# Two unused tiles in SBUF shift the first bytes of a float32r network's weights and activations

## The chip, the core and the metric

The kernel runs on one NeuronCore of a Trainium2 chip. What counts is the device time of one execution in microseconds (us). In the profile PE is TensorE's matmul row, PEld its weight load, DVE VectorE, ACT ScalarE, POOL GpSimd and SP SyncE, whose queue issues the DMAs.

## The reference

One sequence of 256 tokens with 1,024 features goes through two blocks, all in float32. The first block is a feed forward, a hybrid mixer (attention with a forget gate beside a gated delta rule), an attention over a memory of 256 tokens, and a second feed forward. The second block has two layers, each of a feed forward, a mixer (a gated short convolution beside a state space scan), a feed forward and a gated embedding. Cut to what most of the time goes into:

```python
def rms_norm(x, gain):
    xf = x.astype(jnp.float32)
    y = xf * lax.rsqrt(jnp.mean(xf * xf, axis=-1, keepdims=True) + EPS)
    return (y * gain.astype(jnp.float32)).astype(x.dtype)

def swiglu(x, w_gate, w_up, w_down):          # [256,1024] @ [1024,2816], and back
    return (jax.nn.silu(x @ w_gate) * (x @ w_up)) @ w_down

f = swiglu(rms_norm(h, ffn1_pre_norm[l]), ffn1_w_gate[l], ffn1_w_up[l], ffn1_w_down[l])
h = h + FFN_RESIDUAL_WEIGHT * rms_norm(f, ffn1_post_norm[l])
mixed = hybrid_mixer(rms_norm(h, mix_pre_norm[l]), w_in[l], ...)
h = h + rms_norm(mixed @ w_out[l], mix_post_norm[l])
...
return rmsnorm(h, final_norm)
```

There are six such feed forwards and about as much again in the mixers' projections. Each weight is read from memory once.

## The kernel before

**Tiling.** Activations lie with features on the 128 partitions and the 256 tokens along the free axis. A weight unit is 128 partitions by up to four row chunks of 256 columns. It is taken by `wunit` (L283): one DMA into `raw` (L296), a rounding copy into `hi` on ACT (L297), and the remainder into `lo` on DVE (L298). These are tiles of [128, 1024] float32 (4,096 bytes a partition) in the pool `wp`: four buffers of `raw`, three each of `hi` and `lo`.

**The products.** An activation is likewise kept as two float32r parts in one tile `r` of [128, 2, 256] (2,048 bytes a partition). A product of one weight chunk with one activation chunk is three matmuls (`mm3`): hi with the high part, hi with the low part, lo with the high part. Each is a matmul of 256 moving columns with its own load of 128 columns of weights, issued by `mm` at L265. In the profile `pm<-r,hi` means: into a PSUM tile `pm`, the moving operand from an `r` tile, the weights from a `hi` tile. Where weights were loaded ahead (`preload`) they lie in `r` tiles too, and the row reads `pm<-r,r`; where tokens are to stand on the partitions (`proj_tok`) the parts change places, and it reads `pm<-hi,r`. `px<-r,smw` is a product with a few columns of weights (32 or 64 of 128) from a tile `smw`. Matmuls of plain float32 on small tiles are `px<-con,rk` (the identity in `con` moves; the weights are one column of `rk`, repeated), `px<-d,s` and `px<-s,d`; `px<-con,s` at L268 are transposes.

**Order.** A scheduler puts the instructions in order when the program is built; weight units are taken `AHEAD` = 60 places early.

**Where tiles lie.** A pool's tiles are laid one behind another in SBUF, rounded up to 32 bytes, pool after pool: `cst` (constants), `wp` (weights), `sc` (scratch: `sq`, `acc`, `rb`, `t`, `w`, small vectors), `arena` (36 tiles `s` of [128, 256] float32, 20 tiles `r`), and behind these the tiles of a part of the network (`scope`: more `r`, `s` and `d` tiles, 22 `r` tiles in a feed forward). All tiles of `wp` and `arena` have sizes that are multiples of 1,024 bytes, so one pool's tiles all begin at the same remainder of 128, and so do the slices of 512 or 1,024 bytes that matmuls read of them. The pools are opened at L145 to L149, and `mhalf` at L170 is the last constant that is laid down before the products begin.

Of the kernel before, what the change touches and what calls it, by code (L numbers as in the profile page):

```python
# [8 lines left out]
F32 = mybir.dt.float32  # L9
# [6 lines left out]
P = 128  # L16
S = 256
D = 1024
KC = D // P
# [4 lines left out]
# columns of the packed per-feature vectors (one column per 128 features)  # L24
# [10 lines left out]
# rows that every partition holds  # L35
# [54 lines left out]
# how many places of the program order a weight unit is taken ahead, how many one that preload() takes,  # L90
# and how many places products that wait for other engines are put back
# [5 lines left out]
class Arena:  # L97
    """fixed tiles, handed out and taken back in program order"""
# [6 lines left out]
    def add(self, pool, n):  # L105
        """n more tiles from pool, which are handed out first"""
        new = []
        for _ in range(n):
            nm = f"{self.name}{self.n}"
            new.append(pool.tile(self.shape, self.dtype, tag=nm, name=nm, bufs=1)[:])  # L110
            self.n += 1
        self.free[:0] = new
        self.parts.append(new)
# [7 lines left out]
    def get(self, keep=False):  # L121
        """keep: a tile that outlives the parts added last"""
        n = len(self.parts[-1]) if keep and len(self.parts) > 1 else 0
        late = {id(t) for t in self.parts[-1]} if n else ()
        k = [i for i, t in enumerate(self.free) if id(t) not in late]
        assert k, f"arena {self.name} is full"
        t = self.free.pop(k[0])
        self.used[id(t)] = t
        self.peak = max(self.peak, len(self.used))
        return t  # L130
# [6 lines left out]
class Net:  # L137
    def __init__(self, ctx, tc, a):
        self.tc, self.nc, self.a = tc, tc.nc, a
        nc = self.nc  # L140

        def pool(name, bufs, **kw):
            return ctx.enter_context(tc.tile_pool(name=name, bufs=bufs, **kw))

        self.cst = pool("cst", 1)  # L145
        self.wp = pool("wp", 3)
        self.scr, self.parts, self.pp = {}, [], []
        self.sc = pool("sc", 2)
        ap = pool("arena", 1)  # L149
        self.S = Arena("s", [P, S], F32)  # L150
        self.S.add(ap, 36)
        self.R = Arena("r", [P, 2, S], F32R)
        self.R.add(ap, 20)
        self.D = Arena("d", [P, 2, S], F32)
        self.D.add(ap, 0)
        self.pm = pool("pm", 4, space=bass.MemoryType.PSUM)
        self.px = pool("px", 4, space=bass.MemoryType.PSUM)

        self.con = self.cst.tile([P, NCON], F32, name="con")
        self.vec = self.cst.tile([P, NPACK], F32, name="vec")  # L160
        self.ones = {n: self.cst.tile([P, 1], F32, name=f"ones{n}") for n in (1, 128, 512, 1024)}
        nc.gpsimd.memset(self.ones[1], 1.0)
        for n in (128, 512, 1024):
            self.act(self.ones[n], self.ones[1], AF.Copy, scale=1.0 / n)
        self.h = self.start()
        self.ident = self.c("ident")
        nc.sync.dma_start(self.ident, a["con"][:, :P])
        self.ones_sq = self.cst.tile([P, P], F32, name="ones_sq")
        nc.gpsimd.memset(self.ones_sq, 1.0)
        self.mhalf = self.cst.tile([P, 16], F32, name="mhalf")  # L170
        nc.gpsimd.memset(self.mhalf, -0.5)

    def constants(self):
# [7 lines left out]
        # masks and selectors, exact in bfloat16  # L181
# [11 lines left out]
    def start(self):  # L193
        """the activations in the order that the first products need them, with the first weights between"""
# [30 lines left out]
    def t(self, tag, shape, dtype=F32, bufs=2, part=False):  # L225
        """scratch: the next of bufs fixed tiles; part: only there within the current scope"""
        pool, scr = self.parts[-1] if part else (self.sc, self.scr)
        if tag not in scr:
            scr[tag] = [[pool.tile(shape, dtype, tag=f"{tag}{i}", name=f"{tag}{i}", bufs=1)
                         for i in range(bufs)], 0]  # L230
        r = scr[tag]
        r[1] += 1
        return r[0][r[1] % len(r[0])][:]

    def half(self):
        """scratch [P, 256]: halves of the two t tiles in turn"""
# [11 lines left out]
    def late(self, *names):  # L248
        """products that wait for other engines, put behind others that are ready"""
        return self.tc.high_priority(-sum(LATE[n] for n in names))  # L250
# [32 lines left out]
    def wunit(self, src, a, prio=True, cut=1):  # L283
        """hi/lo parts of src [P, a, 256], in cut pieces"""
# [3 lines left out]
        n = a * S  # L288
# [13 lines left out]
    def first(self, *src):  # L302
        """the units that come first when the first blocks of src are taken in step"""
        return [(q, 0, ks) for ks in self.steps(KC) for q in src]

    def preload(self, *units):
        """the parts of units (src, block, row chunks), which are the next to be used, in tiles of the arena"""
# [10 lines left out]
    def units(self, src, b, K):  # L318
        """the weight units of column block b of src [blocks, P, K, 256]: row chunks, hi/lo parts"""
# [13 lines left out]
    def steps(K):  # L333
        """the row chunks of each weight unit"""
        return [range(k, min(k + 4, K)) for k in range(0, K, 4)]

    def block(self, src, b, x, banks):
        """two out chunks in step, so that each weight unit is used up at once"""
# [7 lines left out]
    def proj(self, src, b0, nblk, x, evict, wide=False, last=False):  # L346
        """evict(chunk, ps) with ps [P, 256]: out features on partitions; wide: the first two blocks in step;
        last: the chunks of the last block one after the other"""
# [20 lines left out]
    def proj_tok(self, src, b0, nblk, x, evict):  # L369
        """evict(blk, t, ps) with ps [P, 256]: tokens of tile t on partitions"""  # L370
# [19 lines left out]
    def sq_acc(self, acc, src):  # L390
        """acc + src*src for src [P, 256] (acc None to begin)"""
# [7 lines left out]
    def rstd(self, acc, n, mult=1.0):  # L399
        """[P tokens, 2] of (mean + eps)^-1/2 / sqrt(mult) from tiles of squares or a pair of means in PSUM"""  # L400
# [15 lines left out]
    def spread(self, r, cols=(0, 1)):  # L416
        """PSUM [P, 256]: token values r[:, cols] along the free axis, same on every partition"""
# [21 lines left out]
    def sum_squares(self, ps, h, c):  # L439
        """mean square of the chunks, summed by the tensor engine"""  # L440
# [17 lines left out]
    def scope(self, r, d, s):  # L458
        """more tiles for one part of the network: r float32r pairs, d float32 pairs, s singles"""
# [48 lines left out]
    def residual(self, h, scale):  # L508
        """evict that adds scale*ps to h in place"""
# [4 lines left out]
    def post(self, gain, mult):  # L514
        """evict that keeps gain*f and the squares; then finish adds the normalised f to h"""
# [14 lines left out]
        def finish(h, gain):  # L530
            """also returns the parts of gain*h and the squares for the norm that follows"""
# [13 lines left out]
    def softplus(self, x, shape):  # L545
        """x is a small SBUF tile; returns log(1 + exp(x))"""
# [19 lines left out]
    def three(self, ps, n, tag):  # L566
        """bf16 tile [96, n]: the float32 rows of ps (three copies of 32) in three exact parts"""
# [12 lines left out]
    def small_cols(self, src, n, x, rb=None):  # L580
        """token-major [P, 2, n] of x (times rb) by the few columns of src [P, KC, n]"""
# [3 lines left out]
        # both parts of the columns side by side  # L585
# [22 lines left out]
    def conv(self, y, x, taps, K):  # L608
        """y = causal convolution of x [P, 256] with K taps (columns), bias already folded by the caller"""
# [4 lines left out]
    def mixer1(self, h, x, acc):  # L614
# [55 lines left out]
        # k normalised  # L670
# [17 lines left out]
        # token-major gates  # L688
# [40 lines left out]
        # output norm and gate of the delta rule heads  # L729
# [26 lines left out]
    def gdn(self, kq, vT, g, beta, nbeta):  # L756
        """the outputs, their mean squares, and what runs the delta rule for a few heads"""
# [19 lines left out]
        def run(heads):  # L777
            for hd in heads:
# [22 lines left out]
                # token-major keys and values  # L801
# [12 lines left out]
                # the strictly lower part takes the place of the keys  # L814
# [6 lines left out]
                # q scaled by its decay, in place  # L821
# [85 lines left out]
    def fox(self, fq, fk, fvt, nls):  # L907
# [10 lines left out]
        def run(hd, out):  # L918
            """head hd, split into its half of out"""
# [67 lines left out]
    def mem_attn(self, x, acc):  # L987
# [11 lines left out]
        def weights(hd):  # L999
            """softmax of the head's scores, transposed: [P memory, 2, 256 tokens]"""  # L1000
# [47 lines left out]
    def mixer2(self, h, i, pool):  # L1048
# [39 lines left out]
        # gated short convolution  # L1088
# [76 lines left out]
    def ssd(self, sm, xbc, L):  # L1165
# [28 lines left out]
        def decay(grp, c):  # L1194
            """cb times the decay within the chunks for a pair of heads, transposed"""
# [78 lines left out]
    def ple_proj(self, i):  # L1274
        """the embeddings' part, which no activation comes into"""
# [133 lines left out]
def _arrays(inputs):  # L1409
    """the inputs laid out for the chip: feature-major activations, small vectors packed by partition"""  # L1410
# [22 lines left out]
    def blocks(w):  # L1433
        """[..., K, N] as [..., N/256, P, K/P, 256]: one run of memory per partition and column block"""
# [40 lines left out]
```

## Time and profile before

| | us |
|---|---|
| runs | 2216.78, 2227.3, 2217.13 |
| median of the runs | 2217.13 |
| span of the profiled execution | 2217.7 |

The span runs from the first to the last instruction of the one execution that was profiled. The runs are whole executions; the profiled one has no run time of its own beside its span, which lies 0.6 us above the median. PE is busy for 99% of the span, PEld for 97%, DVE for 70%, ACT for 53%, and the 16 DMA engines for 53%. A busy PE says little by itself, because matmuls overlap each other: how far apart they start is what shows the pace, that is the length of a stretch divided by the matmuls in it.

### The profile page before, as it was taken

The page shows a single profiled execution, that of the slowest core. Times are in us where ns is not written, and L with a number is a line of the kernel's source. Part 1 is how long each engine was busy: PE and PEld are TensorE (multiplying, and loading weights), DVE is VectorE, ACT ScalarE, POOL GpSimd, SP SyncE. Part 2 cuts the span into 40 slices and gives each one's busy share as a digit, 9 for nine tenths or more (in the row PEclk, how much of TensorE's full clock was granted, in tenths as well). Part 3 has the DMA queues.
Part 4 walks back from the last instruction along what each step waited for, and adds up shares of the span by engine and source line. Part 5 has one row for each costly group of instructions (what it writes and reads, how often), then busy time and mean ns, then how long its engine had stood idle before and what let it go on. Part 6 is the DMA issues. An engine that isn't in the chain of part 4 may idle for free.

```text
span 2217.7 us, 45480 instructions
## 1 busy us (share of the span) xinstructions
PE 2195.2 (99%) x18672; PEld 2152.2 (97%) x18672; DVE 1558.5 (70%) x2608; ACT 1185.1 (53%) x2033; POOL 43.3 (2%) x54
## 2 busy tenths in 40 slices
PE   8999999999999999999999999999999999999998
PEld 8999997999999999998999999999999999999998
DVE  6756873667665766798766766676669886767666
ACT  6545633555454544567555554454457755645444
POOL 0000000000000000000000000000000000000000
PEclk9999997999999999999999999999999999999999
DMA  7565520435556556553455556655665436555563
GB/s 255 177 185 169 166 77 1 166 121 162 189 184 191 173 188 186 186 186 106 157 189 185 192 190 195 190 182 195 190 196 187 136 125 193 179 193 193 193 188 127
DMA packets 110369, 379.44 MB, mean 171 GB/s; under 512 B 12368, under 2 KB 17104, under 8 KB 110160
## 3 DMA queue, kind: packets, MB, share of 16 engines
q1 hardware_dynamic: 110160, 376.53, 52.9%
q8 instruction: 146, 2.39, 0.4%
q14 instruction: 63, 0.52, 0.1%
HBM read 375.43 MB, written 1.05 MB: 170 GB/s over the span
## 4 chain that ended last, share of the span: by engine, by line
PE 95%; DVE 2%; ACT 1%; DMA 1%; issue 0%; POOL 0%; SPq 0%; DVEq 0%; ACTq 0%; POOLq 0%
PE pm L265 84%; PE px L265 11%; PE px L268 1%; DVE lo L298 1%; DVE s L259 0%; DMA raw<-in_ffn_w_up_dram 0%; DMA raw<-in_ple_w_gate_dram 0%; ACT hi L297 0%; DMA raw<-in_ffn_wu_dram 0%; DVE r L259 0%; ACT d L262 0%; PE pm L268 0%; ACT L262 0%; DVE acc L256 0%; DVE w L253 0%
## 5 line engine op out<-in xcount | busy, mean ns | idle before, releaser
L265 PE MATMUL pm<-r,hi 128*128 128x256 f32 x10640 | 1861.5, 279 | 7.2 <-ACT hi L297 5.7
L265 PEld LDWEIGHTS pm<-r,hi 128*128 128x128 f32 x10640 | 1621.7, 189 | 9.5 <-ACT hi L297 5.7
L265 PE MATMUL pm<-r,lo 128*128 128x256 f32 x5320 | 1484.4, 279 | 1.6 <-DVE lo L298 1.6
L298 DVE TENSOR_TENSOR lo<-raw,hi 128x1024 fp32r<-128x1024 f32 (+1 forms) x718 | 861.0, 1200 | 488.3 <-ACT hi L297 484.4
L297 ACT CAST hi<-raw 128x1024 fp32r<-128x1024 f32 (+1 forms) x718 | 739.1, 1030 | 731.5 <-PE pm L265 576.5
L265 PEld LDWEIGHTS pm<-r,lo 128*128 128x128 f32 x5320 | 1001.4, 188 | 3.2 <-DVE lo L298 2.2
L276 ACT CAST r<-w 128x256 fp32r<-128x256 f32 x136 | 54.5, 403 | 61.0 <-DVE w L253 61.0
L253 DVE TENSOR_TENSOR t<-pm,rb 128x512 f32<-128x512 f32 (+1 forms) x132 | 80.4, 636 | 0.2
L262 ACT ACTIVATE r<-s,vec 128x256 fp32r<-128x256 f32 x136 | 66.1, 504 | 22.1 <-DVE s L259 18.2
L262 ACT ACTIVATE sq<-s 128x256 f32<-128x256 f32 x152 | 60.3, 410 | 27.6 <-DVE s L253 19.8
L259 DVE SCALAR_TENSOR_TENSOR s<-pm,vec,s 128x255 f32<-128x255 f32 x144 | 68.9, 479 | 2.8
L259 DVE SCALAR_TENSOR_TENSOR r<-s,vec,r 128x256 fp32r<-128x256 f32 x136 | 65.5, 499 | 5.0 <-ACT r L262 4.4
L265 PE MATMUL px<-r,hi 128*128 128x256 f32 x384 | 66.9, 279 | 0.0
L277 DVE TENSOR_TENSOR r<-w,r 128x256 fp32r<-128x256 f32 x136 | 57.0, 422 | 8.1
L265 PEld LDWEIGHTS px<-r,hi 128*128 128x128 f32 x384 | 58.5, 189 | 0.0
L265 PE MATMUL px<-r,lo 128*128 128x256 f32 x192 | 53.5, 278 | 0.0
L413 POOL TENSOR_TENSOR rs<-rv,mhalf 128x2 f32<-128x2 f32 x26 | 23.4, 898 | 1504.2 <-DVE rv L411 1504.2
L262 ACT ACTIVATE w<-t 128x256 f32<-128x256 f32 x132 | 48.1, 409 | 7.1 <-DVE t L253 7.1
L253 DVE TENSOR_TENSOR w<-w,t 128x256 f32<-128x256 f32 x132 | 50.1, 418 | 0.3 <-ACT w L262 0.2
L265 PE MATMUL px<-d,d 128*64 128x128 f32 (+2 forms) x384 | 42.7, 291 | 0.2
L256 DVE TENSOR_TENSOR acc<-acc,sq 128x256 f32<-128x256 f32 x94 | 39.4, 420 | 4.4 <-ACT sq L262 1.9
L262 ACT ACTIVATE d<-px,nac 128x128 f32<-128x128 f32 x128 | 36.4, 375 | 3.2 <-PE px L265 2.9
(231 smaller groups left out, 1371.8 us busy)
## 6 DMA issues: line engine op xcount, KB each, us to landing
raw<-in_w_in_dram SPq DMA_DIRECT2D x188, 512.0 KB, 3.8
raw<-in_ffn_wg_dram SPq DMA_DIRECT2D x88, 512.0 KB, 4.5
raw<-in_ffn_wu_dram SPq DMA_DIRECT2D x88, 512.0 KB, 4.5
raw<-in_ffn_wd_dram SPq DMA_DIRECT2D x80, 512.0 KB, 4.0
raw<-in_ffn_w_up_dram SPq DMA_DIRECT2D x44, 512.0 KB, 4.5
raw<-in_ffn_w_gate_dram SPq DMA_DIRECT2D x43, 512.0 KB, 4.6
raw<-in_ffn_w_down_dram SPq DMA_DIRECT2D x40, 512.0 KB, 3.6
raw<-in_m_w_out_dram SPq DMA_DIRECT2D x32, 512.0 KB, 4.4
```

Source lines behind the costliest of these rows:

```text
L253: self.nc.vector.tensor_tensor(out=out, in0=a, in1=b, op=ALU.mult)
L256: self.nc.vector.tensor_tensor(out=out, in0=a, in1=b, op=ALU.add)
L259: self.nc.vector.scalar_tensor_tensor(out=out, in0=a, scalar=s, in1=b, op0=op0, op1=op1)
L262: self.nc.scalar.activation(out, a, f, **kw)
L265: self.nc.tensor.matmul(out, lhsT=lhsT, rhs=rhs, start=start, stop=stop)
L268: self.nc.tensor.transpose(out, a, self.ident[:k, :k])
L276: nc.scalar.copy(hi, src)
L277: nc.vector.tensor_tensor(out=lo, in0=src, in1=hi, op=ALU.subtract)
L297: nc.scalar.copy(o, r)
L298: nc.vector.tensor_tensor(out=d, in0=r, in1=o, op=ALU.subtract)
L413: self.nc.gpsimd.tensor_tensor(out=r, in0=v, in1=self.mhalf[:, :2], op=ALU.pow)
```

## The change

Two tiles that nothing reads or writes are added. `pad` of [128, 8] float32 (32 bytes a partition) goes into `cst` behind `mhalf`; `pad2` of [128, 16] float32 (64 bytes) goes into `sc` as its first tile. The rest of the diff turns comments and docstrings into empty lines, which shifts line numbers by one or two.

```diff
@@ -146,6 +146,7 @@
         self.wp = pool("wp", 3)
         self.scr, self.parts, self.pp = {}, [], []
         self.sc = pool("sc", 2)
+        self.sc.tile([P, 16], F32, name="pad2", bufs=1)
         ap = pool("arena", 1)
         self.S = Arena("s", [P, S], F32)
         self.S.add(ap, 36)
@@ -168,6 +169,7 @@
         self.ones_sq = self.cst.tile([P, P], F32, name="ones_sq")
         nc.gpsimd.memset(self.ones_sq, 1.0)
         self.mhalf = self.cst.tile([P, 16], F32, name="mhalf")
+        self.cst.tile([P, 8], F32, name="pad")
         nc.gpsimd.memset(self.mhalf, -0.5)
```

In the built programs the instructions of every engine stand in the same order before and after, with the same operands and the same waits; there are 23,676 of them on the engines. Only addresses differ. The first byte of the tiles, as a remainder of 128:

| tiles | before | after |
|---|---|---|
| `raw`, `hi`, `lo` | 96 | 0 |
| `r`, `s`, `d` (arena and parts), `smw` | 32 | 0 |
| `sq`, `acc`, `rb`, `t`, `w` | 96 | 64 |
| `con` (identity and triangles) | 0 | 0 |

## Rows read from the trace of the kernel before

**Rows 1.** The page: busy us, share of the span, instructions, of four engines
```profile
PE 2195.2 (99%) x18672; PEld 2152.2 (97%) x18672; DVE 1558.5 (70%) x2608; ACT 1185.1 (53%) x2033; POOL 43.3 (2%) x54
```

**Rows 2.** The chain that ended last, shares of the span by engine
```profile
PE 95%; DVE 2%; ACT 1%; DMA 1%; issue 0%; POOL 0%; SPq 0%; DVEq 0%; ACTq 0%; POOLq 0%
```

**Rows 3.** The chain's longest pieces in order of time: start us, us, what, matmuls
```profile
34.43 23.08 PE pm L265 x196
...
60.76 141.33 PE pm L265 x1200
...
545.29 11.31 PE px L265 x96
556.59 164.18 PE pm L265 x1394
...
753.20 170.89 PE pm L265 x1451
...
943.38 65.04 PE pm L265 x572
...
1065.87 86.99 PE pm L265 x767
...
1192.85 80.37 PE pm L265 x709
...
1278.34 10.88 PE px L265 x96
1289.22 147.98 PE pm L265 x1306
...
1495.29 164.45 PE pm L265 x1451
...
2024.92 163.64 PE pm L265 x1443
```

**Rows 4.** Two stretches of feed forward: busy us (instructions), granted clock, DMA share, GB/s
```profile
754.00:924.00 170.00, 170.00 (x1447) 170.00 (x1445) 1.00 0.60 186
...
1496.00:1659.00 163.00, 163.00 (x1440) 163.00 (x1439) 1.00 0.61 193
```

**Rows 5.** Groups by line and shape, of matmuls with float32r operands
```profile
L265 PE MATMUL pm<-r,hi 128*128 128x256 f32 x10640 | 1861.5, 279 | 7.2 <-ACT hi L297 5.7 <-DVE r L259 0.9 <-ACT r L262 0.6
...
L265 PE MATMUL pm<-r,lo 128*128 128x256 f32 x5320 | 1484.4, 279 | 1.6 <-DVE lo L298 1.6
```

**Rows 6.** PE in order of time, 1471 us on: start us, us to the last end, what
```profile
1471.13 5.92 PE L265 MATMUL pm<-r,r 128*128 128x256 f32 x48
1476.89 0.28 PE L265 MATMUL pm<-r,hi 128*128 128x256 f32 x1
```

**Rows 7.** Matmuls with few weight columns, and their weight loads (min/median/max ns)
```profile
940.60 1.99 PE L265 MATMUL px<-r,smw 128*64 128x256 f32 x16
...
L265 PEld LDWEIGHTS px<-r,smw x48: 107/134/135, 223.1 to 1677.8; 128*64 128x64 f32 x32, 128*32 128x32 f32 x16
```

**Rows 8.** Plain float32 of 128 columns: PEld at 253 us, PE at 305 us
```profile
253.25 1.86 PEld L265 LDWEIGHTS px<-con,rk 128*128 128x128 f32 x16 [0.65 <-POOL rk L675]
...
305.20 0.39 PE L265 MATMUL px<-d,s 128*128 128x128 f32 x2
...
306.99 0.28 PE L265 MATMUL px<-d,d 128*128 128x128 f32 x1
```

**Rows 9.** Nine transposes in order of time on PE
```profile
1026.27 1.15 PE L268 MATMUL px<-con,s 128*128 128x128 f32 x9
```

**Rows 10.** Groups on DVE and ACT by shape: busy us, mean ns, idle before
```profile
L298 DVE TENSOR_TENSOR lo<-raw,hi 128x1024 fp32r<-128x1024 f32 x684 | 837.7, 1225 | 458.4 <-ACT hi L297 454.5
L297 ACT CAST hi<-raw 128x1024 fp32r<-128x1024 f32 x684 | 718.1, 1050 | 685.6 <-PE pm L265 536.2 <-issue 104.8 <-PE px L265 20.4
...
L253 DVE TENSOR_TENSOR w<-w,t 128x256 f32<-128x256 f32 x132 | 50.1, 418 | 0.3 <-ACT w L262 0.2
...
L256 DVE TENSOR_TENSOR s<-s,s 128x256 f32<-128x256 f32 x48 | 19.3, 420 | 0.5
```

**Rows 11.** The chain's longest piece that is a DMA
```profile
4.01 6.40 DMA raw<-in_ffn_w_up_dram
```

## The prediction, made before the change was run

> **What bounds the kernel now.** I read the busy shares first: PE and PEld are full, DVE and ACT are not [rows 1]. Then the chain of work that ended last: 95% of the span lies on PE [rows 2]. So the time is a number of matmuls times the pace at which they follow each other, plus a few stalls. The chain's longest pieces give that pace, length over count [rows 3]. They fall into two classes. Up to 924 us: 23.08/196, 141.33/1200, 164.18/1394 and 170.89/1451 are all 117.8 ns. Later, 147.98/1306, 164.45/1451 and 163.64/1443 are 113.3 to 113.4 ns, and the pieces from 943, 1066 and 1193 us, which are met again in the second layer, 113.4 to 113.7 ns. The mean duration of 279 ns, which is the same for hi and lo [rows 5], hides this; only starts show it.
>
> What differs between the classes? Not the clock: it is granted in full, which is 2.4 GHz, in a stretch of either class, and the DMA share is 0.60 and 0.61 [rows 4]. Not the code: these two are the same feed forward of layers 0 and 1. Not the remainders of 128 of the addresses, which are the same in both. So one layout allows two steady paces, and something earlier decides which one holds.
>
> Then the rows where addresses do differ. 48 matmuls with weights in `r` tiles start over 1476.89 - 1471.13 = 5.76 us, that is 120.0 ns each [rows 6], and the long stretches on either side of them run at 113.3. Shape, type and order are those of the hi/lo triples; only the weights begin at remainder 32 instead of 96. Addresses therefore matter to TensorE.
>
> In columns at 2.4 GHz (0.4167 ns each), 113.3 ns is 272 = 17 x 16, 120.0 is 288 = 18 x 16, and 117.8 is 282.7, the mean of 17, 18 and 18 times 16. A matmul has 256 = 16 x 16 columns. Sixteen float32 columns are 64 bytes of a partition, and 1,024 bytes that begin at a remainder of 32 touch 17 blocks of 64 bytes. My reading, an inference from these three paces: at this rate the moving operand comes in blocks of 64 bytes, a block touched in part costs as much as a whole one, and the weight load beside it costs another in some stretches. The 17th block isn't the weight load's doing: with 32 or 64 weight columns, whose loads are short (107 to 135 ns), the 256 columns still go at (1.99 - 0.28)/15 = 114 ns [rows 7].
>
> **The change part by part.** Instructions, order and waits are the same, so nothing is added to any queue, and the two unused tiles cost no time. What is left is what an address does to each user.
>
> *TensorE.* After the change moving operand and weights begin at 0, so 16 blocks instead of 17. The next floor is the weight load. The plain float32 products show it: 16 loads of 128 columns in 1.86 us, (1.86 - 0.19)/15 = 111.3 ns, where the weights are one repeated column, and 16 matmuls from 305.20 to 306.99 us, 111.9 ns each, where they are tiles at remainder 32 [rows 8]. Both kinds of operand give the same, so I take 111.6 ns as a floor that doesn't hang on the address. Bounds: transposes, whose moving operand `con` begins at 0, run at (1.15 - 0.27)/8 = 110 ns [rows 9], the lower end; the upper end is the 120.0 of [rows 6].
>
> *A rule.* The matmuls follow each other at 113.3 at best in these rows. The Trainium skill, "TensorE: Matmul & The Clock Gate", Back-to-back issue gap, gives N/2.4 + 2.5 ns for a warm stream, 109.2 ns for 256 columns. The trace disagrees by 4.1 ns; by that rule the gain below would be about 99 us.
>
> *DVE and ACT.* The same DVE operation takes 418 ns on scratch at remainder 96 and 420 ns on `s` tiles at 32 [rows 10]. I put nothing for them, and either sign under 1% is hidden: `lo` waits 454 us for ACT, and ACT's `hi` 536 us for PE. If PE goes at 111.6, a unit of 24 matmuls lasts 2.68 us, against 1.05 for its `hi` and 1.23 for its `lo` [rows 10]: still covered.
>
> *DMA.* Only about 1% of the span's chain is DMA [rows 2], its longest piece 6.4 us at the start [rows 11]. Bounds of plus or minus 1 us; I take 0.
>
> *The sum.* How many matmuls lie in each class? In float32r there are 17,040: 10,640 + 5,320 [rows 5] and 1,080 in smaller groups. The pieces of [rows 3] hold 4,241 at 117.8 and, with the second layer's three repeats, 8,296 at 113.3; six `px` pieces of 96 or 100, one in each feed forward, add 292 to the first (11.31/96 = 117.8) and 288 to the second (10.88/96 = 113.3). The other 3,923 lie in short pieces of both paces; I halve them. So about 6,490 at 117.8 and 10,550 at 113.3. At 111.6: 6,490 x 6.2 = 40.2 us and 10,550 x 1.7 = 17.9 us, together 58.1 us. 2217.7 - 58.1 = 2159.6 for the span, and with the 0.6 us by which the span exceeds the median, **2159 us**. What is late next is still PE, now held by its weight loads.
>
> **The rivals.**
>
> *Only the extra block goes (faster).* Aligned operands keep one block too many, from the start of a stream or the weight load, but never two: 113.3 everywhere. 6,490 x 4.5 = 29.2, so 2188 us. For it: 113.3 is the pace even beside short weight loads. Against: no reason for a 17th block is left.
>
> *No block but the bare stream (faster).* The pace of the transposes, which their row gives as 109 to 110 [rows 9]; at 109.5 it is 6,490 x 8.3 + 10,550 x 3.8 = 94 us, 2123 us. The transposes speak for it, the 111.3 of the loads against it.
>
> *Nothing hangs on the remainder of 64 or 128.* Both paces stay where they are, 2217 us. For it: the two share one layout. Against: the 120.0. The Trainium skill, "SBUF — State Buffer", Specifications, speaks of cachelines of 16 bytes with a penalty for crossing into a new one; all tiles begin at multiples of 32 already, so by it the change would do nothing. The 120.0 doesn't follow from lines of 16 bytes alone.
>
> *Equal remainders collide (slower).* In [rows 6] moving operand and weights have equal remainders, 32 and 32, while in the triples they are 32 and 96. If it is this meeting of two reads that costs the 18th block, and the 17th is there whatever the address, the change brings it to every triple: 120.0 everywhere, 10,550 x 6.7 + 6,490 x 2.2 = 85 us, 2302 us. It decides if the 17th block isn't due to the part block. Against: 16 + 1 would be 113.3 if the 17th goes.
>
> *The 117.8 takes over (slower).* The two paces stay, but the new addresses start every stretch in the longer one: 10,550 x 4.5 = 47 us, 2264 us.
>
> **How the numbers follow.** About 0.5% (11 us) is what a measurement here can tell from no change. Forecast (111.6) 0.36, extra block only 0.20, bare stream 0.06: faster 0.62. Nothing: 0.14. Collision 0.14, all at 117.8 0.10: slower 0.24. The likeliest case alone would be 2150 to 2175. For 8 in 10 the range needs the forecast, the 2188, no change and the 117.8 everywhere; it leaves out the bare stream and the collision: 2150 to 2266.
>
> **What would show it.** The long pieces of the chain, divided out as above: 111 to 112 ns in all of them, first and second half alike, says the forecast; 113.3 in all, the extra block; 109, the bare stream; two classes again, no effect; 120, the collision. The 48 `pm<-r,r` matmuls should no longer differ from their neighbours if blocks are the cause, since all remainders are then 0. DVE, ACT and DMA rows should keep their durations. The prediction is wrong if the stretches at 113.3 stay there or get longer, or if the weight load's floor turns out to hang on the address.

## The result, and the profile after

The changed kernel takes 2289.03 us (median of four runs, 2288.69 to 2294.22). Against the kernel before on the same chip (median of four runs 2222.22) the ratio is 1.03, 95% interval [1.0266, 1.0334]: slower, and outside the range. Its profiled execution has a span of 2286.9 us, 69.2 more than the 2217.7 before.

The page of the kernel after, busy us of four engines, and below it the shares of the chain that ended last. They answer [rows 1, 2]:

```profile
PE 2268.3 (99%) x18672; PEld 2229.0 (97%) x18672; DVE 1562.2 (68%) x2608; ACT 1183.4 (52%) x2033; POOL 43.5 (2%) x54
...
PE 97%; DMA 1%; DVE 1%; ACT 1%; issue 0%; SPq 0%; POOL 0%; DVEq 0%; ACTq 0%; POOLq 0%
```

PE is busy for 73.1 us more, with the same 18,672 instructions; DVE and ACT stay within 4 us of where they were. So the time sits in the pace of the matmuls. The longest pieces of the chain of the kernel after, in order of time (start us, us, what, matmuls), answer [rows 3]:

```profile
61.42 143.98 PE pm L267 x1200
...
547.16 11.52 PE px L267 x96
558.68 167.28 PE pm L267 x1394
...
758.67 174.12 PE pm L267 x1451
...
952.29 68.83 PE pm L267 x572
...
1078.81 92.08 PE pm L267 x767
...
1529.46 174.12 PE pm L267 x1451
...
2084.30 173.16 PE pm L267 x1443
```

Length over count is 120.0 ns in every one of them (120.3 in 572, which has a few other matmuls between). The two classes of before, 117.8 and 113.3, are gone, and neither is left anywhere in the long pieces. Two stretches of feed forward in the kernel after (busy us of PE, PEld, DVE, ACT and POOL with their instructions, granted clock, DMA share, GB/s), the same layers as in [rows 4]:

```profile
760.00:930.00 170.00, 170.00 (x1419) 170.00 (x1419) 106.53 (x140) 80.98 (x119) 2.56 (x1) 1.00 0.58 183
1531.00:1701.00 170.00, 170.00 (x1419) 170.00 (x1418) 106.55 (x141) 80.89 (x119) 2.56 (x1) 1.00 0.58 183
```

The clock is granted in full as before, and the DMA moves slightly less per second (183 GB/s against 186 and 193), which fits a PE that uses up weights more slowly. The groups by line and shape of the kernel after (busy us, mean ns, idle before), beside [rows 5, 10]:

```profile
L267 PE MATMUL pm<-r,hi 128*128 128x256 f32 x10640 | 1939.6, 284 | 6.5 <-ACT hi L299 5.7 <-DVE r L261 0.6 <-ACT r L264 0.2
...
L300 DVE TENSOR_TENSOR lo<-raw,hi 128x1024 fp32r<-128x1024 f32 x684 | 837.5, 1224 | 512.7 <-ACT hi L299 510.6
L299 ACT CAST hi<-raw 128x1024 fp32r<-128x1024 f32 x684 | 715.4, 1046 | 757.6 <-PE pm L267 580.2 <-issue 129.0 <-PE px L267 22.3
```

DVE's `lo` takes 1224 ns (1225 before), ACT's `hi` 1046 (1050); both idle longer, `hi` for PE above all. Of these engines only PE became slower.

### The profile page after: what moved, and what is told of

Its sections match the earlier page's. It is cut to its first block, busy times and chain, and to the rows that moved or that the text cites. A ratio compares the mean times of both kernels' runs of the same rounds, so it can differ in the third digit from the quotient of the medians.

```text
span 2286.9 us, 45480 instructions
## 1 busy us (share of the span) xinstructions
PE 2268.3 (99%) x18672; PEld 2229.0 (97%) x18672; DVE 1562.2 (68%) x2608; ACT 1183.4 (52%) x2033; POOL 43.5 (2%) x54
## 4 chain that ended last, share of the span: by engine, by line
PE 97%; DMA 1%; DVE 1%; ACT 1%; issue 0%; SPq 0%; POOL 0%; DVEq 0%; ACTq 0%; POOLq 0%
PE pm L267 86%; PE px L267 11%; PE px L270 1%; DMA raw<-in_ple_w_gate_dram 0%; DMA raw<-in_ffn_w_up_dram 0%; DMA raw<-in_ffn_wu_dram 0%; PE pm L270 0%; ACT d L264 0%; ACT hi L299 0%; DVE lo L300 0%; ACT L264 0%; POOL rs L415 0%; DVE s L255 0%; ACT r L264 0%; DVE r L279 0%
## 5 line engine op out<-in xcount | busy, mean ns | idle before, releaser
L267 PE MATMUL pm<-r,hi 128*128 128x256 f32 x10640 | 1939.6, 284 | 6.5 <-ACT hi L299 5.7
L267 PEld LDWEIGHTS pm<-r,hi 128*128 128x128 f32 x10640 | 1665.5, 192 | 8.9 <-ACT hi L299 5.7
L267 PE MATMUL pm<-r,lo 128*128 128x256 f32 x5320 | 1510.8, 284 | 0.3 <-DVE lo L300 0.3
L267 PEld LDWEIGHTS pm<-r,lo 128*128 128x128 f32 x5320 | 1022.7, 192 | 1.5 <-issue 0.7
L267 PE MATMUL px<-r,hi 128*128 128x256 f32 x384 | 69.5, 283 | 0.0
```

The lines of the kernel that those rows point to most:

```text
L267: self.nc.tensor.matmul(out, lhsT=lhsT, rhs=rhs, start=start, stop=stop)
```

## Experiments: own remainders, or the difference of two addresses?

In what follows the **difference** of a matmul is the first byte of the tile that moves less the first byte of the tile of its weights, modulo 256. Where `r` moves and `hi` or `lo` are the weights, it is 192 before the change, for `hi` and `lo` alike, and 0 after it. The 48 matmuls `pm<-r,r`, whose two operands are `r` tiles of 2,048 bytes, have 0 in both kernels. The diffs are against the kernel after where it is named, otherwise against the kernel before.

**One half of the change alone.** First only `pad` (against after), which puts the weights at remainder 0 of 128 and `r` at 64:

```diff
-        self.sc.tile([P, 16], F32, name="pad2", bufs=1)
```

> Only the 32 unused bytes behind the constants: weights (hi, lo) begin at remainder 0 of 128, activations (r) at 64. Theory 'difference': what counts is whether the moving operand and the weights begin at the same remainder of 128; here they differ by 64, as before the change, so the paces of before come back, 113.3 and 117.8 ns, and the time lies between 2185 and 2265 us. Theory 'own place': weights that begin at 0 (or 32) cost the 18th block wherever the activations are; then 120.0 ns everywhere and 2287 to 2302 us. Theory 'part blocks' (the prediction's): both operands begin at a multiple of 64, so no more than 113.3 ns anywhere, 2188 us or less.

Then only `pad2` (against after), both at remainder 96:

```diff
-        self.cst.tile([P, 8], F32, name="pad")
```

> Only the 64 unused bytes behind the scratch: weights and activations both at remainder 96. Theory 'difference': equal remainders, so 120.0 ns everywhere and about 2289 us as with both tiles, although no operand begins at a multiple of 64. Theory 'own place': weights lie where they lay before the change, so 113.3 and 117.8 ns and 2185 to 2265 us. Theory 'part blocks': as before the change, 2217 to 2228 us.

With the weights at 0 and `r` at 64: 2219.62 us, ratio 1.0014 [0.9994, 1.0034]. Its long chain pieces:

```profile
554.58 164.18 PE pm L266 x1394
...
751.18 170.90 PE pm L266 x1451
...
1494.71 164.45 PE pm L266 x1451
...
2026.87 163.64 PE pm L266 x1443
```

That is 117.8, 117.8, 113.3 and 113.4 ns, the two paces of before, although both operands now begin at multiples of 64. No block is touched in part any more, and the better pace is still 113.3, the time of 272 columns. With both at 96: 2293.9 us, 1.0355 [1.0326, 1.0384], and the long pieces of that kernel are

```profile
561.36 167.28 PE pm L266 x1394
...
761.36 174.12 PE pm L266 x1451
...
1531.28 174.12 PE pm L266 x1451
```

120.0 in all. Here `r`, `hi` and `lo` all begin off the multiples of 64, and the pace is that of the kernel after. So it isn't where either operand begins that counts, but how far they lie apart: 192 in the first, as before; 0 in the second, as after.

**How far apart, and modulo what?** Six kernels change the size of the second unused tile, and with it the difference; two of them make constants smaller too. Their matmuls and the order of these are those of before; only addresses differ. Difference 32 (against after):

```diff
-        self.sc.tile([P, 16], F32, name="pad2", bufs=1)
+        self.sc.tile([P, 24], F32, name="pad2", bufs=1)
```

> Both tiles, but 96 bytes behind the scratch instead of 64: weights at remainder 0, activations at 32 as before the change. Theory 'difference': unequal remainders, so not 120.0 throughout; with a difference of 32 that no row has shown, between 111.6 and 117.8 ns, 2160 to 2265 us. Theory 'own place': weights at 0, so 120.0 ns and 2287 to 2302 us.

Difference 224 (against after):

```diff
-        self.sc.tile([P, 16], F32, name="pad2", bufs=1)
+        self.sc.tile([P, 8], F32, name="pad2", bufs=1)
```

> Both tiles, but 32 bytes behind the scratch instead of 64: weights at remainder 0, activations at 96. Theory 'difference': unequal remainders, so not 120.0 throughout, between 111.6 and 117.8 ns and 2160 to 2265 us; if the sign of the difference counts, another time than with activations at 32. Theory 'own place': weights at 0, so 120.0 ns and 2287 to 2302 us.

Difference 128, so that the remainders of 128 are equal and those of 256 not:

```diff
+        self.sc.tile([P, 48], F32, name="pad2", bufs=1)
...
-        self.mhalf = self.cst.tile([P, 16], F32, name="mhalf")
+        self.mhalf = self.cst.tile([P, 8], F32, name="mhalf")
```

> Activations and weights both at remainder 64 of 128, but 128 apart of 256 (pad out, mhalf 8 columns, pad2 48 columns). Theory 'difference of 128': only the remainder of 128 counts, so 120.0 ns everywhere and about 2290 us. Theory 'difference of 256': tiles 128 apart of 256 do not meet, so another pace, 113.3 ns or less, 2190 us or less.

Difference 64 (against after):

```diff
-        self.sc.tile([P, 16], F32, name="pad2", bufs=1)
+        self.sc.tile([P, 32], F32, name="pad2", bufs=1)
```

> Activations begin 64 after the weights of 256, where before the change they begin 64 before them (192 of 256); pad kept, pad2 128 bytes. Theory 'difference of 128': the two are the same, so 113.3 and 117.8 ns in long stretches, as before, 2185 to 2265 us. Theory 'difference of 256': another pace in all stretches, which continues the row 120.0, 116.7 at differences 0 and 32: near 113.3 ns throughout, 2190 us.

Difference 96, and 160:

```diff
+        self.sc.tile([P, 40], F32, name="pad2", bufs=1)
```

> Activations begin 96 after the weights of 256 (pad out, pad2 160 bytes). So far, difference of 256 and pace: 0: 120.0, 32: 116.7, 64: 113.3 and 117.8, 128: 118.7, 192: 113.3 and 117.8, 224: 118.3. Theory 'distance from a meeting': the pace rises again from 64 to 128, so 115 to 119 ns throughout, 2205 to 2275 us. Theory 'one good place': the two paces at 64 come from lying at an edge, and 96 is free of meetings, so 113.3 ns throughout and about 2188 us.

```diff
+        self.sc.tile([P, 56], F32, name="pad2", bufs=1)
...
-        self.ones = {n: self.cst.tile([P, 1], F32, name=f"ones{n}") for n in (1, 128, 512, 1024)}
+        ones = self.cst.tile([P, 8], F32, name="ones")
+        self.ones = {n: ones[:, i:i + 1] for i, n in enumerate((1, 128, 512, 1024))}
...
-        self.mhalf = self.cst.tile([P, 16], F32, name="mhalf")
+        self.mhalf = self.cst.tile([P, 8], F32, name="mhalf")
```

> Activations begin 160 after the weights of 256, which is 96 before them (pad out, mhalf 8 columns, the four ones in one tile, pad2 224 bytes). Theory 'distance from a meeting': 115 to 119 ns throughout, 2205 to 2275 us. Theory 'one good place': 113.3 ns throughout and about 2188 us.

What was measured; the pace is length over count of the pieces with 1,443 or 1,451 matmuls:

| difference | kernel | pace, ns | median, us | ratio [95%] |
|---|---|---|---|---|
| 0 | after | 120.0 | 2289.03 | 1.03 [1.0266, 1.0334] |
| 0 | w96_r96 | 120.0 | 2293.9 | 1.0355 [1.0326, 1.0384] |
| 32 | w0_r32 | 116.7 | 2239.23 | 1.0118 [1.0087, 1.015] |
| 64 | plus64 | 113.4 and 117.8 | 2230.57 | 1.0061 [1.0022, 1.01] |
| 96 | plus96 | 120.0 | 2291.8 | 1.0339 [1.03, 1.0379] |
| 128 | plus128 | 118.7 | 2271.18 (two runs) | 1.023 [1.0192, 1.0268] |
| 160 | minus96 | 118.7 | 2270.87 | 1.0245 [1.0209, 1.0282] |
| 192 | before, w0_r64 | 113.3 and 117.8 | 2217.13, 2219.62 | w0_r64: 1.0014 [0.9994, 1.0034] |
| 224 | w0_r96 | 118.3 | 2272.38 | 1.0261 [1.0231, 1.0291] |

One chain piece of each from the second half. Difference 32:

```profile
1498.27 169.29 PE pm L267 x1451
```

Difference 224:

```profile
1518.80 171.70 PE pm L267 x1451
```

Difference 128:

```profile
1515.98 172.18 PE pm L266 x1451
```

Difference 64, where both paces are met again in one execution, 117.8 and 113.4:

```profile
1491.64 170.90 PE pm L267 x1451
...
2032.94 163.70 PE pm L267 x1443
```

Difference 96:

```profile
1532.88 174.12 PE pm L266 x1451
```

Difference 160:

```profile
1515.06 172.19 PE pm L267 x1451
```

Three things follow. Modulo 128 isn't enough: differences of 0 and 128 are the same there, and run at 120.0 and 118.7. The pace isn't a distance from a single meeting point: 96 is as bad as 0, and lies between the best, 64, and 128; for 96 a pace of 115 to 119 had been expected, and 120.0 came. And no difference brings a pace below 113.3. Two more expectations missed: at 224 at most 117.8 had been expected, at 128 either 120.0 or no more than 113.3. The map is measured, not explained: I have no rule that gives all eight numbers.

The same executions hold the map a second time, with the parts exchanged. In `proj_tok` a `hi` or `lo` tile moves and the weights lie in an `r` tile, so the difference changes its sign: 32 becomes 224, 224 becomes 32, 160 becomes 96. The first 96 of these matmuls, from their first start to the next row, in w0_r32, w0_r96 and minus96:

```profile
288.62 0.40 PE L267 MATMUL pm<-hi,r 128*128 128x256 f32 x2
...
299.98 0.38 PE L267 MATMUL pm<-con,nls 128*96 128x128 f32 x2
...
292.01 0.40 PE L267 MATMUL pm<-hi,r 128*128 128x256 f32 x2
...
303.21 0.38 PE L267 MATMUL pm<-con,nls 128*96 128x128 f32 x2
...
290.05 0.40 PE L267 MATMUL pm<-hi,r 128*128 128x256 f32 x2
...
301.56 0.38 PE L267 MATMUL pm<-con,nls 128*96 128x128 f32 x2
```

That is 11.36, 11.20 and 11.51 us over 96: 118.3, 116.7 and 119.9 ns, where the table has 118.3, 116.7 and 120.0 for 224, 32 and 96. So the sign of the difference counts (32 and 224 are not alike), and which of the two tiles moves does not. One stretch strays: in plus96, where the sign makes 160 of 96, the first 96 go at 118.7 and the next 96 at 117.4. It also shows that 256 is enough as the modulus here: by the addresses in the built programs, the 96 of minus96 is 96 modulo 512 too, while the 96 of plus96 in the table is 352.

**The order of the three products.** In the kernel before, `hi` is loaded twice in a row. Here `lo` goes between:

```diff
-        self.mm(ps, wh, xl, False, False)
-        self.mm(ps, wl, xh, False, last)
+        self.mm(ps, wl, xh, False, False)
+        self.mm(ps, wh, xl, False, last)
```

> The layout of before, but the three matmuls of a product in the order hi with high part, lo with high part, hi with low part. Theory 'same load twice': the 117.8 ns pace comes from loading the same hi columns twice in a row, which no longer happens, so 113.3 ns throughout and about 2188 us. Theory 'start of a stretch': which pace holds is decided by how a stretch begins and not by the order within the triple, so both paces stay, 2185 to 2265 us.

2222.72 us, 1.0027 [1.0006, 1.0048]. Both paces stay, 117.8 and 113.3, as two of its chain pieces show:

```profile
750.83 170.90 PE pm L265 x1451
...
1496.05 164.45 PE pm L265 x1451
```

So the longer pace doesn't come from loading the same weights twice in a row.

**The kernel before once more**, unchanged, to see which stretches take which pace:

> The kernel before, unchanged, profiled once more. Theory 'fixed by the program': each long stretch has the pace that it had in the first profile, 117.8 ns in the first three feed forwards and 113.3 in the last three, and a span within 2 us of 2217.7. Theory 'chance at the start of a stretch': some long stretches change their pace, by 4.4 ns a matmul, which is 5 to 7 us for a feed forward; that would be the spread of the runs from 2207 to 2228 us.

2227.41 us in this execution, near the upper end of what the kernel before gave in all (2207.39 to 2228). Two of its chain pieces:

```profile
1493.82 170.90 PE pm L265 x1451
...
1684.00 67.57 PE pm L265 x572
```

In [rows 3] the first, at 1495.29 us, took 164.45 us; now it goes at 117.8. The second repeats the 65.04 us of 943.38 and went at 113.7; now it goes at 118.1. Same program, same layout, same place, another pace: it is not fixed by the program, and once taken it holds through a stretch. These two pieces alone take 9.0 us more, and the spans differ by 7.9 (2225.6 against 2217.7). So such changes can make the spread of the kernel before, 19.8 us in 15 runs on one chip, and 11.2 in four on the chip on which four runs of the kernel after keep to 5.5; that they make all of it isn't shown.

**Different differences for `hi` and `lo`.** An unused tile between `hi` and `lo` in the pool of the weights, made when the first weight unit is set up. With 128 bytes the difference of `hi` is 64 and that of `lo` 192:

```diff
+        if not hasattr(self, "pad3"):
+            self.pad3 = self.wp.tile([P, 32], F32, tag="pad3", name="pad3", bufs=1)
```

> An unused tile of 128 bytes between hi and lo, and neither pad: activations begin 64 after hi and 192 after lo of 256, the two differences at which both 113.3 and 117.8 ns were seen. Theory 'each pair by itself': nothing changes, both paces, 2205 to 2230 us. Theory 'lock of three': 117.8 is a pattern that three equal differences in a row keep up; broken by lo, 113.3 ns throughout and about 2188 us, below both kernels.

With 64 bytes `hi` has 0 and `lo` 192:

```diff
+        if not hasattr(self, "pad3"):
+            self.pad3 = self.wp.tile([P, 16], F32, tag="pad3", name="pad3", bufs=1)
```

> An unused tile of 64 bytes between hi and lo, and neither pad: activations begin at the same remainder of 256 as hi (difference 0) and 192 after lo. Theory 'each pair by itself': two of three matmuls at 120.0 and one at 113.3, a mean of 117.8 ns throughout and about 2255 to 2265 us. Theory 'lock of three': one meeting holds up all three, 120.0 ns throughout and about 2290 us.

With 128 bytes: 2192.74 us, 0.9894 [0.9858, 0.9929], which beats both kernels; its slowest run, 2199.18, is faster than every run of the kernel before. Its chain pieces:

```profile
724.05 10.88 PE px L265 x96
734.93 164.45 PE pm L265 x1451
...
1457.69 10.88 PE px L265 x96
1468.57 164.45 PE pm L265 x1451
...
1997.08 163.71 PE pm L265 x1443
```

113.3 to 113.5 in both halves; every feed forward runs at the better of the two paces. It isn't 113.3 everywhere. In a part of a mixer, PE of the same kernel in order of time (start us, us to the last end, what):

```profile
914.78 0.28 PE L265 MATMUL pm<-r,lo 128*128 128x256 f32 x1
...
915.85 0.28 PE L265 MATMUL pm<-r,lo 128*128 128x256 f32 x1
915.96 1.98 PE L265 MATMUL px<-r,smw 128*64 128x256 f32 x16
```

Ten matmuls start over 915.96 - 914.78 = 1.18 us, 118 ns each. A step is the time from one start to the next. Of the 16,713 steps of 105 to 128 ns behind float32r matmuls with 128 columns of weights, 1,761 last over 116 ns in this kernel; at some 5 ns each that is about 9 us, enough for the distance from the 2188 of 113.3 everywhere to the 2193 measured.

With 64 bytes: 2255.98 us, 1.0167 [1.0127, 1.0208]. Its chain pieces:

```profile
743.58 11.31 PE px L265 x96
754.89 170.89 PE pm L265 x1451
...
1502.42 11.31 PE px L265 x96
1513.73 170.90 PE pm L265 x1451
```

117.8 throughout, and 117.8 is (120.0 + 120.0 + 113.3)/3: two products of a triple have `hi` with difference 0, one has `lo` with 192. Each pair costing what its own difference says, with the costs added, gives this number; but it is also that of the longer pace at 192. The single steps speak for the second: in some 5,300 triples the steps behind `hi`, `hi` and `lo` average 117.6, 117.5 and 118.3 ns, and not 120.0, 120.0 and 113.3. Nor do the two kernels bear out one theory together: each pair by itself gave lo64's number and missed lo128's, a lock of three missed lo64's and nearly gave lo128's.

## Why the prediction was wrong, by its own steps

**The bound: right.** The time is a number of matmuls times a pace, and the whole change lies there. From the starts of all matmuls in the records: the 16,447 steps of 105 to 128 ns behind float32r matmuls that move an `r` tile over 128 columns of weights sum to 1892.9 us before and 1972.6 after, +79.7. Steps of over 128 ns, which hold the waits, shrink by 12.7 us (167.1 to 154.4), all others add 2.5: together +69.5, against +69.2 of the span. That a PE which takes longer lets DVE and ACT be ready in time, and so wins back those 12.7 us, fits the longer idle time of DVE and ACT, but no run isolated it.

**The failed step: the 17th block as a part block.** From three paces the prediction inferred that a moving operand at remainder 32 touches one block of 64 bytes too many, and that aligning it takes that block away. What the runs showed in its place: aligned operands keep the paces of before (w0_r64: 113.3 and 117.8), and what the change did was to move the difference from 192 to 0, where the pace is 120.0 at either remainder tried (0 in after, 96 in w96_r96). The row on which the inference rested keeps its pace too. PE of the kernel after in order of time, answering [rows 7]:

```profile
949.51 1.99 PE L267 MATMUL px<-r,smw 128*64 128x256 f32 x16
951.34 0.40 PE L267 MATMUL pm<-r,hi 128*128 128x256 f32 x2
```

Sixteen starts over 951.34 - 949.51 = 1.83 us are 114 ns, as before, with every address now at remainder 0. So aligning took no block away, and no layout tried has a long stretch below 113.3; the forecast of 111.6 had no block to remove. Why 256 columns take the time of 272 at best stays open. The Trainium skill, "TensorE: Matmul & The Clock Gate", Back-to-back issue gap, whose formula gives 109.2 for 256 columns, wasn't reached in any of the layouts either; the section calls it the gap of an isolated matmul and gives other spacings for a stream with weight loads, which the prediction left out.

**The refused rival was the one.** "Equal remainders collide" was given 0.14 and named its own point of decision, that the 17th block isn't due to the part block; that is what happened. It was refused by the argument that failed (16 + 1 would be 113.3). Its 85 us were for 17,040 matmuls; the pace did cost 79.7 over the 16,447 steps, where the same working gives 82. In spans its 2217.7 + 85 is 15.8 us above the 2286.9 measured: some 5 of pace and 13 of waits that it left out, less 2.5 of other matmuls. "Remainders" was half right: it is the difference modulo 256 that counts, equal remainders of 128 with a difference of 128 cost less, 118.7, and unequal ones with a difference of 96 cost as much, 120.0. So its time came true; that two reads meet is not shown by that.

**The test with the 48 matmuls didn't tell the theories apart.** PE of the kernel after around them, answering [rows 6]:

```profile
1505.12 5.92 PE L267 MATMUL pm<-r,r 128*128 128x256 f32 x48
1510.88 0.40 PE L267 MATMUL pm<-r,hi 128*128 128x256 f32 x2
```

1510.88 - 1505.12 = 5.76 us, 120.0 ns each. They no longer differ from their neighbours, as the prediction asked, but because the neighbours came up to them. It should have asked which of the two moves. Before the change this was the one row with the geometry that the change would bring to every triple and with loads of 128 columns, and it stood at 120.0. The `px<-r,smw` of [rows 7] have a difference of 0 as well, in both kernels, and go at 114 beside loads of 64 columns: a difference of 0 alone doesn't make 120.0.

**The weight load's floor: held, and never reached.** PEld of the kernel after, answering [rows 8]:

```profile
257.36 1.86 PEld L267 LDWEIGHTS px<-con,rk 128*128 128x128 f32 x16
```

(1.86 - 0.19)/15 = 111.3 ns as before; float32r matmuls don't come down to it, so no run shows whether it would bound them.

**DVE, ACT, DMA at nothing: right.** Their rows keep their durations, as the groups above show.

**Nothing hangs on the remainder: wrong for this change.** The prediction set beside it the Trainium skill, "SBUF — State Buffer", Specifications, whose lines of 16 bytes would leave all layouts here alike. They aren't, at 113.3 to 120.0. The same page, Who interferes with whom, gives TensorE two independent read ports, one for the moving operand and one for the weight load, and says that it never waits on anyone. The runs speak against that independence as far as these two operands go: with `r` at remainder 64 of 128 the pace was 113.3 and 117.8, 118.7, or 120.0, according to a difference of 192, 128 or 96 (w0_r64, plus128, plus96). That the two reads meet in a part of the memory is my reading of this; the runs show only the dependence.

**What stays open.** Why differences of 64 and 192 allow two paces, when the others tried hold one in their long stretches; and why different differences for `hi` and `lo`, 64 and 192, hold the feed forwards at the better one. One layout shows the latter, and its short stretches at 118 to 119 don't follow from it. What the two reads share, if they do, no run shows.

## What to carry to other kernels

Look among the rows of before for one that already has the geometry that a change brings, and price the change by it ahead of any reading of why; a test that both theories pass, as that of the 48 matmuls, is no test. Alignment of each operand is not a virtue in itself here: what counted was the distance between the moving operand and the weights, and bringing all tiles to multiples of 128 bytes set it to 0, the worst value beside 96, for every product of `hi` and `lo`. Where matmuls are bound by their pace, take it from starts, length over count, in several executions: where one program shows two paces, an unused tile that changes the distances is worth a trial (it gave 1.1% here).

## What the runs showed of the hardware that was not expected

- The pace of float32r matmuls of 128 x 128 by 256 columns hangs on the distance, modulo 256 bytes, from weights to moving operand: 120.0 ns at 0 and 96, 118.7 at 128 and 160, 118.3 at 224, 116.7 at 32, and 113.3 or 117.8 at 64 and 192, all at a granted clock of 1.00, which is 2.4 GHz. With the roles of the tiles exchanged, 224, 32 and 96 gave 118.3, 116.7 and 119.9.
- With 192 the pace changes between executions of the same program at the same place (164.45 or 170.90 us for the same 1,451 matmuls); with 64 both paces were met in one execution.
- With differences of 64 for `hi` and 192 for `lo` the long stretches all ran at 113.3 to 113.5, in the one layout of that kind that was tried.
